# A hybrid mixer and MoE step on one core: another order in the first norm, four modulation sums moved, additions handed to GpSimd

## The chip, the cores and the metric

The kernel runs on one core of a Trainium2 chip. The metric is the device time of one execution in microseconds, lower is better. TensorE multiplies matrices, VectorE and ScalarE work on tiles elementwise, GpSimd does a few elementwise operations and issues some DMAs, SyncE issues most DMAs. In the profile they are PE (its weight loads: PEld), DVE, ACT, POOL and SP.

## The reference, cut to what matters

One layer for 128 context tokens and 1024 latent tokens of width 1024, all in fp32:

```python
mod = silu(c) @ w_mod + b_mod                 # 6 vectors of 1024, for context and latent each
shift1, scale1, gate1, shift2, scale2, gate2 = split(mod, 6)
hn = rmsnorm(x, norm1) * (1 + scale1) + shift1
u = hn @ w_in                                 # p (512), v (1024), g1 (1024), g2 (1024)
y_pool = pool_mixer(p)                        # 4 windows, one 128x128 product each
v = conv4(v)                                  # along the tokens
r, i = sigmoid(v @ w_r + b_r), sigmoid(v @ w_i + b_i)   # 2 directions, 16 heads of 64
a = exp(-8 * r * softplus(-lam)); h = scan(a * h + sqrt(1 - a^2) * i * v)
y_lru = h_forward + h_backward
merged = sigmoid(g1) * (y_pool @ w_br_pool) + sigmoid(g2) * (y_lru @ w_br_lru)
x = x + gate1 * (merged @ w_out)
x = x + gate2 * moe(rmsnorm(x, norm2) * (1 + scale2) + shift2)   # 16 experts, expert choice
y = rmsnorm(x, final_g)
```

## The kernel before

The program is written out by hand in one order (`manual_schedule`); each engine gets its instructions in the order in which the Python code emits them, and waits are set where tiles depend on each other. Products of fp32 matrices are done in halves: `split` (L181) copies a weight into `hi` in a rounded format on ScalarE (L188) and takes the remainder `lo` on VectorE (L189), and `mm3` (L197) adds three products on TensorE. A product of a 1024x128 block of `w_in` with all 1152 tokens (`dense`, L280) is 72 matmuls into one of two PSUM tiles.

**The list.** All weights of the first part stand in one list `seq` (L221 to L236): 18 items of the head, then v(2), g2(2), ... with one modulation sum m(n) behind each item, 28 in all, and bl(0) to bl(7) at the end. Behind v(7) come g1(0), g2(7), p(0) to p(3). `do_split(n)` (L269) splits the items up to number n that are not split yet and issues the loads some items further ahead; there are four buffers for `hi` and `lo` each and three for raw weights.

**The head.** The tokens are normalised, transposed, and modulated by scale1 and shift1, one channel block k of eight after the other. The modulation's first 2048 columns come in 16 blocks a(0) to a(15), four to a quarter q. `mod_first` multiplies one block; the blocks in `DP` are multiplied as plain fp32 with the vectors in `sil4`, the others in halves. `mod_low` copies a quarter's sums out of PSUM, `mod_second` transposes them by small products (L401) and adds the bias (L405). `hn_first(k)` and `hn_cols(k)`, `hn_low(k)` modulate block k and split it (L354 to L370), and `dense_v(j, k)` multiplies it for v(0) and v(1) at once.

**The gates.** For each j, `conv(j)` convolves v on VectorE, `gates(j)` does the four gate products of 9 matmuls (TensorE) with a Sigmoid each (ScalarE), `gates_rest(j)` is a chain of Tanh, Exp, Square, Sqrt on ScalarE and products on VectorE, and `scans(j)` does the scans and their split on VectorE. In the main loop (L722) an item v(j) is followed by its `gates(j - 1)`, `conv(j)`, a `do_split(i + 5)` and `gates_rest(j - 1)`. The last of them hang on g1(0): its product, its Sigmoid (`gate_evac`), `scans(6)`, `gates(7)`, `do_split(i + 5)`, and `gates_rest(7)` behind the next m. In this way the order at the end of the gates is, with what is split at each place:

```
v(7) m10 gates(6) conv(7) [split g2(7)] gates_rest(6)
g1(0) scans(6) gates(7) [split m12, p(0)] m11 gates_rest(7) [split m13]
g2(7) scans(7) ...
```

**The modulation sums.** `mod_block` (L660) does the 8 products of one m(n) into a PSUM tile that two neighbours share; behind the second, ScalarE copies it (L669), and five items later `mod_cols` (L209) transposes it on TensorE (L213) and adds on VectorE (L217, L218). Such postponed steps are in `later` and are taken at the head of the loop, ahead of the item's product. The transposes and sums take turns in two PSUM tiles.

**The pooling.** `pool_evac(g)` (L609) copies p(g) out of PSUM on ScalarE, calls `pool_mm(g - 1)` and does a chain of additions on VectorE.

**The projection.** `project(i, h)` (L955) multiplies tile i of 128 tokens with half h of `w_out`; VectorE multiplies by gate1 (L980) and adds the input rows (L981), which SyncE loads into a tile of two in turn, behind the norm's stores in its queue. Then come the second norm (`norm2`, L1005), the router, and steps of the routing (`affinities`, `first_cols`, `first_row`, `part_ranks`, `prompt_b`) hung on given products. After that the 16 experts' weights are streamed.

Of the kernel before, what the change touches and what calls it, by code (L numbers as in the profile page):

```python
# [8 lines left out]
F32 = mybir.dt.float32  # L9
# [17 lines left out]
FL, FM = 0, 0  # L27
DP = range(4)
T = SP + SL
# [20 lines left out]
def hybrid_step_kernel(ctx: ExitStack, tc: tile.TileContext, x_prompt, x_sample, state_lru, c, c_ctx,  # L50
# [69 lines left out]
    pk = const.tile([P, 16], F32, name="pk")  # L120
    l_a = ini.tile([P, 16], F32, name="l_a")
    l_e = ini.tile([P, 16], F32, name="l_e")
    l_z = ini.tile([P, 16], F32, name="l_z")
    l_q = ini.tile([P, 16], F32, name="l_q")

# [103 lines left out]
    full = [("v", 0), ("v", 1), ("g2", 0), ("g2", 1)]  # L229
    for n, jb in enumerate(seq[4:]):  # L230
        full.append(jb)
        if n < 32 - 2 * NGT:
            full.append(("m", n))

# [116 lines left out]

    def hn_cols(k):
        for x, z in ((xv[:, k, 0, :SP], 0), (xv[:, k, 0, SP:], 1), (xv[:, k, 1:], 1)):
            V.tensor_scalar(x, x, s1[:, z, k:k + 1], modc[:, 0, z, k:k + 1], op0=OP.mult, op1=OP.add)  # L354
        A.copy(hn_hi[:, k, :].rearrange("p (g t) -> p g t", g=3), xv[:, k])

# [36 lines left out]
    def mod_low(q):  # L393
        mrow1[q] = xsp.tile([P, D], F32, name="mrow1", tag="junk")[:4, :512]
        A.copy(mrow1[q][:, :256], mps[q][:4, :256])
        (A.copy if q else V.tensor_copy)(mrow1[q][:, 256:], mps[q][:4, 256:])

# [30 lines left out]
    go1(slice(6, 9))  # L428
    do_split(4)
    norm1(2)  # L430
    x_cols1(1, 0, A)
    x_cols1(1, 1, A)
    mod_first(0)
    mod_first(1)
    x_cols1(2, 0, V)
    x_cols1(2, 1, A)
    mod_first(2)
    mod_first(3)
    mod_low(0)
    do_split(5)  # L440
    mod_second(0)
    turn[0] += FL
    va = [acc_tile(), acc_tile()]
    hn_first(0)
    do_split(8)

    for q in range(4):
        k = 2 * q
        if q < 3:
            do_split(4 * q + 10)  # L450
        dense_v(0, k)
        for n in (4, 5) if q < 3 else ():
            mod_first(4 * q + n)
        hn_cols(k + 1)
        dense_v(1, k)
        for n in (6, 7) if q < 3 else ():
            mod_first(4 * q + n)
        hn_low(k + 1)
        if q < 3:
            mod_low(q + 1)  # L460
            do_split(4 * q + 12 if q < 2 else HEAD + 2)
        dense_v(0, k + 1)
        if q < 3:
            mod_second(q + 1)
        dense_v(1, k + 1)
        if q < 3:
            hn_first(k + 2)
    softplus()
    do_split(HEAD + 2)
# [17 lines left out]
    G.memset(graw, 0.0)  # L487
    LR = {}

    def load_gates(j):  # L490
# [118 lines left out]
    def pool_evac(g, a3):  # L609
# [5 lines left out]
        for q in range(2):  # L615
            A.copy(lat[:, 4 + 6 * q:10 + 6 * q], a3[:, 1 + q, :CH].rearrange("p (r c) -> p r c", c=GW))
        if g:
            pool_mm(g - 1)
# [85 lines left out]
    later = []  # L704
    rests = []
    load_gates(0)
    v_evac(va[0])
    conv(0)
    for j in range(2):
        do_split(HEAD + 1 + j)  # L710
        a3 = dense(spl.pop(("g2", j)), KD, hn_hi, hn_lo)
        if j == 0:
            v_evac(va[1])
        A.dma_start(g2_d[j], gate_evac(a3))
        if j == 0:
            gates(0)
            conv(1)
            do_split(HEAD + 4)
            gates_rest(0)
        else:  # L720
            scans(0)
    for i in range(HEAD + 2, len(seq)):  # L722
        kind, j = seq[i]
        if kind == "m" and (kind, j) not in spl and i < done_split[0]:
            continue
        if (kind, j) != ("g1", 0):
            do_split(i + 4)
        for d in list(later):
            d[0] -= 1
            if d[0] <= 0:  # L730
                d[1]()
                later.remove(d)
        if kind == "bl" and j == 0:
            mg_hi = pool_sb["dp"].tile([P, KD, T], F32R, name="mg_hi", tag="D")
            mg_lo = big.tile([P, KD, T], F32R, name="mg_lo", tag="H2")
        if kind == "m":
            mod_block(j // 2, j % 2, spl.pop((kind, j)))
            for f in rests:
                f()
            rests = []  # L740
            if j == 31 - 2 * NGT:
                later.append([5, mod_rows])
            continue
# [15 lines left out]
        else:  # L759
            a3 = dense(w, KD, hn_hi, hn_lo)  # L760
        if kind == "g1" and j:
            g1s[j] = gate_evac(a3)
# [3 lines left out]
        if kind == "v":  # L766
            v_evac(a3)
            if seq[i + 1][0] == "m":
                n = seq[i + 1][1]
                mod_block(n // 2, n % 2, spl.pop(("m", n)))  # L770
            gates(j - 1)
# [7 lines left out]
        elif kind == "g1":  # L779
            if j == 0:  # L780
                g1s[j] = gate_evac(a3)
                scans(KD - 2)
                gates(KD - 1)
                do_split(i + 5)
                rests.append(lambda: gates_rest(KD - 1))
            if j == 3:
# [168 lines left out]
    def project(i, h, mid=(), part=False):  # L955
# [24 lines left out]
        V.tensor_tensor(tmp, ps, g1r[z][:, hs], op=OP.mult)  # L980
        V.tensor_tensor(x2s[i][:, hs], x2s[i][:, hs], tmp, op=OP.add)  # L981

# [814 lines left out]
```

## Time and profile before

| | |
|---|---|
| median of 3 runs | 2151.72 us (2150.81 to 2152.35) |
| profiled execution | 2155.95 us |
| its span, first to last instruction | 2154.2 us |
| TensorE busy | 2070.4 us (96%) |
| VectorE busy | 1709.6 us (79%) |
| ScalarE busy | 1358.8 us (63%) |
| GpSimd busy | 190.9 us (9%) |

Times in the profile's rows count from the span's start. A row of a timeline gives start, duration, engine, line, operation, output and inputs, and in brackets how long the engine was idle before and what released it. Matmuls overlap, so the distance of their starts is their cost.

### The profile page before, as it was taken

The page shows a single profiled execution, that of the slowest core. Times are in us where ns is not written, and L with a number is a line of the kernel's source. Part 1 is how long each engine was busy: PE and PEld are TensorE (multiplying, and loading weights), DVE is VectorE, ACT ScalarE, POOL GpSimd, SP SyncE. Part 2 cuts the span into 40 slices and gives each one's busy share as a digit, 9 for nine tenths or more (in the row PEclk, how much of TensorE's full clock was granted, in tenths as well). Part 3 has the DMA queues.
Part 4 walks back from the last instruction along what each step waited for, and adds up shares of the span by engine and source line. Part 5 has one row for each costly group of instructions (what it writes and reads, how often), then busy time and mean ns, then how long its engine had stood idle before and what let it go on. Part 6 is the DMA issues. An engine that isn't in the chain of part 4 may idle for free.

```text
span 2154.2 us, 40533 instructions
## 1 busy us (share of the span) xinstructions
PE 2070.4 (96%) x17269; PEld 1974.4 (92%) x17269; DVE 1709.6 (79%) x1847; ACT 1358.8 (63%) x1444; POOL 190.9 (9%) x324
## 2 busy tenths in 40 slices
PE   6999999999999987899999999999999999999995
PEld 4799998999998875899999999999999999999994
DVE  6788988732236467988988898998998998899896
ACT  6477675321112225677877777877877777777783
POOL 0000001010101001020010010011010011011021
PEclk9999999999999988999999999999999999999997
DMA  8133434174644238699999999999999999999995
GB/s 265 56 118 114 125 111 124 55 223 117 203 158 170 109 110 296 237 326 332 346 328 334 343 331 324 343 340 326 333 335 327 338 341 328 336 341 323 339 313 181
DMA packets 304820, 543.91 MB, mean 252 GB/s; under 512 B 16300, under 2 KB 85628, under 8 KB 304639
## 3 DMA queue, kind: packets, MB, share of 16 engines
q1 hardware_dynamic: 285306, 478.56, 64.0%
q0 software_dynamic: 15728, 52.77, 8.4%
q10 hardware_dynamic: 3604, 9.98, 1.4%
q8 instruction: 135, 2.21, 0.4%
q14 instruction: 47, 0.38, 0.1%
HBM read 500.60 MB, written 40.67 MB: 251 GB/s over the span
## 4 chain that ended last, share of the span: by engine, by line
PE 86%; DVE 8%; DMA 2%; ACT 2%; issue 1%; SPq 0%; DVEq 0%; ACTq 0%
PE ac L1465 37%; PE ac L1473 17%; PE a L198 6%; PE a L199 6%; PE a L200 6%; PE a L757 5%; DVE lo L1280 2%; PE a L984 1%; PE a L986 1%; PE a L985 1%; DMA xg<-hn_d,lgi 1%; PE tp L1404 1%; PE tp L1489 1%; DVE lo L189 1%; PE tp L665 1%
## 5 line engine op out<-in xcount | busy, mean ns | idle before, releaser
L1280 DVE TENSOR_TENSOR lo<-raw,hi 128x2048 bf16<-128x2048 f32 x384 | 870.9, 2281 | 0.0
L1274 ACT CAST hi<-raw 128x2048 fp32r<-128x2048 f32 x384 | 729.4, 1912 | 3.8 <-issue 2.2
L1465 PE MATMUL ac<-x,hi 128*128 128x288 f32 x4096 | 606.1, 300 | 0.0
L1465 PEld LDWEIGHTS ac<-x,hi 128*128 128x128 f32 x4096 | 553.0, 189 | 1.0 <-issue 0.9
L1473 PEld LDWEIGHTS <-lo 128*128 128x128 bf16 x6144 | 380.4, 98 | 36.7 <-DVE lo L1280 0.8
L1465 PE MATMUL ac<-hh,hi 128*128 128x288 f32 x2048 | 332.9, 304 | 0.0
L1478 ACT COPY bs<-ac 128x288 f32<-128x288 f32 x320 | 127.8, 399 | 290.6 <-PE ac L1473 289.1
L1473 PE MATMUL ac<-xb,lo 128*128 128x144 bf16 x4096 | 302.4, 227 | 0.6 <-DVE lo L1280 0.6
L1465 PEld LDWEIGHTS ac<-hh,hi 128*128 128x128 f32 x2048 | 279.9, 189 | 0.0
L198 PE MATMUL a<-hn_hi,hi 128*128 128x384 f32 x624 | 212.0, 340 | 0.0
L199 PE MATMUL a<-hn_lo,hi 128*128 128x384 f32 x624 | 210.8, 338 | 0.0
L200 PE MATMUL a<-hn_hi,lo 128*128 128x384 f32 x624 | 210.8, 338 | 0.0
L1473 PE MATMUL ac<-hb,lo 128*128 128x144 bf16 x2048 | 171.9, 227 | 0.0
L189 DVE TENSOR_TENSOR lo<-raw,hi 128x1024 fp32r<-128x1024 f32 (+1 forms) x76 | 86.7, 1163 | 78.8 <-ACT hi L188 78.2
L1479 DVE TENSOR_TENSOR h<-ac,bs 128x288 f32<-128x288 f32 x256 | 115.7, 452 | 42.1 <-ACT bs L1478 41.8
L198 PEld LDWEIGHTS a<-hn_hi,hi 128*128 128x128 f32 x624 | 117.1, 188 | 0.4
L199 PEld LDWEIGHTS a<-hn_lo,hi 128*128 128x128 f32 x624 | 117.2, 188 | 0.0
L200 PEld LDWEIGHTS a<-hn_hi,lo 128*128 128x128 f32 x624 | 117.2, 188 | 0.0
L1710 POOL TENSOR_TENSOR yps<-ot,modc 128x128 f32<-128x128 f32 x16 | 35.9, 2247 | 735.2 <-DVE ot L1479 735.2
L188 ACT CAST hi<-raw 128x1024 fp32r<-128x1024 f32 (+1 forms) x76 | 74.8, 1001 | 41.2 <-PE a L199 33.3
L1479 DVE TENSOR_TENSOR ot<-ac,bs 128x288 f32<-128x288 f32 x64 | 29.3, 457 | 69.7 <-ACT bs L1478 69.7
L699 ACT ACTIVATE sg<-a 128x1152 f32<-128x1152 f32 x16 | 18.1, 1134 | 82.4 <-PE a L200 82.3
(447 smaller groups left out, 2626.8 us busy)
## 6 DMA issues: line engine op xcount, KB each, us to landing
raw<-in_exp_w_dram SPq DMA_DIRECT2D x380, 1024.0 KB, 7.2
raw<-in_w_in_dram SPq DMA_DIRECT2D x28, 512.0 KB, 5.0
raw<-in_w_mod_dram SPq DMA_DIRECT2D x28, 512.0 KB, 5.3
araw<-in_w_mod_dram SPq DMA_DIRECT2D x18, 256.0 KB, 4.5
g_d<-sg ACTq DMA_DIRECT2D x8, 576.0 KB, 3.2
yh_d<-yh POOLq DMA_DIRECT2D x8, 576.0 KB, 3.1
yl_d<-yl POOLq DMA_DIRECT2D x8, 576.0 KB, 4.6
m_d<-sg POOLq DMA_DIRECT2D x8, 576.0 KB, 4.2
```

Of the source, the lines that this page charges most:

```text
L188: A.copy(h, raw)
L189: V.tensor_tensor(l, raw, h.bitcast(F32), op=OP.subtract)
L198: PE.matmul(out, whi, xhi, start=first, stop=False)
L199: PE.matmul(out, whi, xlo, start=False, stop=False)
L200: PE.matmul(out, wlo, xhi, start=False, stop=last)
L757: PE.matmul(a3[:, ch, :CH], w[:, k, :], y[:, k, cs], start=n == 0 and k == 0 and w is hi, stop=n == 1 and k == KD - 1 and w is ws[-1])
L1274: A.copy(hl[n][0], raw[n])
L1280: V.tensor_tensor(lo, r, hi.bitcast(F32), op=OP.subtract)
L1465: PE.matmul(a[:, r, :2 * S], w[0][:, k, c0 + r * P:c0 + (r + 1) * P], x2(kk), start=kk == first, stop=False)
L1473: PE.matmul(a[:, r, S:2 * S], w[1][:, k, c0 + r * P:c0 + (r + 1) * P], xb(kk), start=False, stop=kk == last)
L1478: A.copy(b, a[:, :, S:2 * S])
L1479: V.tensor_tensor(dst, a[:, :, :S], b, op=OP.add)
```

## The change

- **List.** Four modulation sums instead of one stand behind g1(0); the rest keep their order.
- **Head.** Block a(3) is done in halves. Some `do_split` calls move; `hn_cols` is cut into `hn_mod` and `hn_high`, and `hn_mod` goes ahead of the splits; `mod_low` is one copy on ScalarE, behind the next two splits. `softplus` moves behind `conv(0)`.
- **Main loop.** The position is in `at`, and `sums_next(n)` takes the next n sums from the list where it is called: behind a v's evacuation, inside `pool_evac` ahead of `pool_mm`, and four of them between `scans(6)` and `gates(7)`. `gates_rest(7)` follows `gates(7)` at once. Postponed steps are taken behind an item's product instead of ahead of it.
- **Projection.** The addition of tiles 1 to 7 is done on GpSimd.

```diff
@@ -25,7 +25,7 @@
 NGT = 2
 G0, G1, GX, G2 = 3, 8, 9, 15
 FL, FM = 0, 0
-DP = range(4)
+DP = range(3)
 T = SP + SL
 NT = T // P
 CH = 384
@@ -118,10 +118,6 @@
     lamc = col_a[:, IA["lam"]:IA["lam"] + 16]
     nk = const.tile([P, 16], F32, name="nk")
     pk = const.tile([P, 16], F32, name="pk")
-    l_a = ini.tile([P, 16], F32, name="l_a")
-    l_e = ini.tile([P, 16], F32, name="l_e")
-    l_z = ini.tile([P, 16], F32, name="l_z")
-    l_q = ini.tile([P, 16], F32, name="l_q")
 
     def softplus():
         A.activation(l_a, lamc, AF.Abs)
@@ -227,10 +223,13 @@
         seq += [("g1", j), ("bp", j)]
     seq += [("g1", 6), ("g1", 7), ("bp", 6), ("bp", 7)]
     full = [("v", 0), ("v", 1), ("g2", 0), ("g2", 1)]
-    for n, jb in enumerate(seq[4:]):
+    n = 0
+    for jb in seq[4:]:
         full.append(jb)
-        if n < 32 - 2 * NGT:
-            full.append(("m", n))
+        for _ in range(4 if jb == ("g1", 0) else 1):
+            if n < 32 - 2 * NGT:
+                full.append(("m", n))
+                n += 1
 
     head = [("a", n) for n in range(4)] + [("v", 0), ("v", 1)] + [("a", n) for n in range(4, 16)]
     seq = head + full[2:] + [("bl", j) for j in range(8)]
@@ -349,9 +348,11 @@
         PE.transpose(tpb[:, :n_b], par_b[:n_b], ident[:n_b, :n_b])
         V.tensor_copy(col_b[:, :n_b], tpb[:, :n_b])
 
-    def hn_cols(k):
+    def hn_mod(k):
         for x, z in ((xv[:, k, 0, :SP], 0), (xv[:, k, 0, SP:], 1), (xv[:, k, 1:], 1)):
             V.tensor_scalar(x, x, s1[:, z, k:k + 1], modc[:, 0, z, k:k + 1], op0=OP.mult, op1=OP.add)
+
+    def hn_high(k):
         A.copy(hn_hi[:, k, :].rearrange("p (g t) -> p g t", g=3), xv[:, k])
 
     def hn_first(k):
@@ -392,8 +393,7 @@
 
     def mod_low(q):
         mrow1[q] = xsp.tile([P, D], F32, name="mrow1", tag="junk")[:4, :512]
-        A.copy(mrow1[q][:, :256], mps[q][:4, :256])
-        (A.copy if q else V.tensor_copy)(mrow1[q][:, 256:], mps[q][:4, 256:])
+        A.copy(mrow1[q], mps[q][:4])
 
     def mod_second(q):
         t = tp_tile()
@@ -426,46 +426,48 @@
     sq1(7, 9)
     params()
     go1(slice(6, 9))
-    do_split(4)
+    do_split(3)
     norm1(2)
     x_cols1(1, 0, A)
     x_cols1(1, 1, A)
+    do_split(4)
     mod_first(0)
     mod_first(1)
     x_cols1(2, 0, V)
     x_cols1(2, 1, A)
     mod_first(2)
     mod_first(3)
+    do_split(6)
     mod_low(0)
-    do_split(5)
     mod_second(0)
     turn[0] += FL
     va = [acc_tile(), acc_tile()]
     hn_first(0)
+    hn_mod(1)
     do_split(8)
 
     for q in range(4):
         k = 2 * q
-        if q < 3:
-            do_split(4 * q + 10)
+        if q:
+            hn_mod(k + 1)
+        do_split(4 * q + 10 if q < 3 else HEAD + 2)
         dense_v(0, k)
         for n in (4, 5) if q < 3 else ():
             mod_first(4 * q + n)
-        hn_cols(k + 1)
+        hn_high(k + 1)
         dense_v(1, k)
         for n in (6, 7) if q < 3 else ():
             mod_first(4 * q + n)
         hn_low(k + 1)
         if q < 3:
+            do_split(min(4 * q + 12, HEAD))
             mod_low(q + 1)
-            do_split(4 * q + 12 if q < 2 else HEAD + 2)
         dense_v(0, k + 1)
         if q < 3:
             mod_second(q + 1)
         dense_v(1, k + 1)
         if q < 3:
             hn_first(k + 2)
-    softplus()
     do_split(HEAD + 2)
     spl.pop(("v", 0))
     spl.pop(("v", 1))
@@ -486,6 +488,7 @@
     graw = lp.tile([P, 4, P], F32, name="graw")
     G.memset(graw, 0.0)
     LR = {}
+    l_a, l_e, l_z, l_q = (lp.tile([P, 16], F32, name=f"l{n}") for n in "aezq")
 
     def load_gates(j):
         for m, w in enumerate((lru_wr, lru_wi)):
@@ -614,6 +617,7 @@
         A.copy(lat[:, 0:4], a3[:, 0, SP:CH].rearrange("p (r c) -> p r c", c=GW))
         for q in range(2):
             A.copy(lat[:, 4 + 6 * q:10 + 6 * q], a3[:, 1 + q, :CH].rearrange("p (r c) -> p r c", c=GW))
+        sums_next(1)
         if g:
             pool_mm(g - 1)
         cur, a, b = ppad, 0, PADT
@@ -702,10 +706,10 @@
     g1s = {}
     late = []
     later = []
-    rests = []
     load_gates(0)
     v_evac(va[0])
     conv(0)
+    softplus()
     for j in range(2):
         do_split(HEAD + 1 + j)
         a3 = dense(spl.pop(("g2", j)), KD, hn_hi, hn_lo)
@@ -719,25 +723,40 @@
             gates_rest(0)
         else:
             scans(0)
-    for i in range(HEAD + 2, len(seq)):
-        kind, j = seq[i]
-        if kind == "m" and (kind, j) not in spl and i < done_split[0]:
-            continue
-        if (kind, j) != ("g1", 0):
-            do_split(i + 4)
+
+    def turn_later():
         for d in list(later):
             d[0] -= 1
             if d[0] <= 0:
                 d[1]()
                 later.remove(d)
+
+    def sums_next(n):
+
+        while n and seq[at[0] + 1][0] == "m":
+            at[0] += 1
+            m = seq[at[0]][1]
+            do_split(at[0] + 1)
+            turn_later()
+            mod_block(m // 2, m % 2, spl.pop(("m", m)))
+            if m == 31 - 2 * NGT:
+                later.append([5, mod_rows])
+            n -= 1
+
+    at = [HEAD + 1]
+    while at[0] + 1 < len(seq):
+        at[0] += 1
+        i = at[0]
+        kind, j = seq[i]
+        if (kind, j) != ("g1", 0):
+            do_split(i + 4)
+        if kind == "m":
+            turn_later()
         if kind == "bl" and j == 0:
             mg_hi = pool_sb["dp"].tile([P, KD, T], F32R, name="mg_hi", tag="D")
             mg_lo = big.tile([P, KD, T], F32R, name="mg_lo", tag="H2")
         if kind == "m":
             mod_block(j // 2, j % 2, spl.pop((kind, j)))
-            for f in rests:
-                f()
-            rests = []
             if j == 31 - 2 * NGT:
                 later.append([5, mod_rows])
             continue
@@ -758,6 +777,7 @@
                                       stop=n == 1 and k == KD - 1 and w is ws[-1])
         else:
             a3 = dense(w, KD, hn_hi, hn_lo)
+        turn_later()
         if kind == "g1" and j:
             g1s[j] = gate_evac(a3)
         for f in late:
@@ -765,9 +785,7 @@
         late = []
         if kind == "v":
             v_evac(a3)
-            if seq[i + 1][0] == "m":
-                n = seq[i + 1][1]
-                mod_block(n // 2, n % 2, spl.pop(("m", n)))
+            sums_next(1)
             gates(j - 1)
             conv(j)
             do_split(i + 5)
@@ -780,9 +798,10 @@
             if j == 0:
                 g1s[j] = gate_evac(a3)
                 scans(KD - 2)
+                sums_next(4)
                 gates(KD - 1)
                 do_split(i + 5)
-                rests.append(lambda: gates_rest(KD - 1))
+                gates_rest(KD - 1)
             if j == 3:
                 ppk.close()
                 yhp = pyh.enter_context(tc.tile_pool(name="yhp", bufs=1, reuse_waits="tile"))
@@ -978,7 +997,7 @@
             return
         tmp = tk.tile([P, 512], F32, name="tmp", bufs=2)
         V.tensor_tensor(tmp, ps, g1r[z][:, hs], op=OP.mult)
-        V.tensor_tensor(x2s[i][:, hs], x2s[i][:, hs], tmp, op=OP.add)
+        (G if 0 < i < NT - 1 else V).tensor_tensor(x2s[i][:, hs], x2s[i][:, hs], tmp, op=OP.add)
 
     def mm3_t(out, xhi, xlo, whi, wlo, first, last):
         PE.matmul(out, xhi, whi, start=first, stop=False)
```

## Rows read from the trace of the kernel before

**Rows 1.** Cores; then the page's busy us (share) and instructions.
```profile
core 0: 2154.2 us, clock 0.983
...
PE 2070.4 (96%) x17269; PEld 1974.4 (92%) x17269; DVE 1709.6 (79%) x1847; ACT 1358.8 (63%) x1444; POOL 190.9 (9%) x324
```

**Rows 2.** Stretches: us, busy us by engine, granted clock, DMA share, GB/s.
```profile
769.00:775.00 6.00, 5.64 (x26) 4.85 (x27) 3.92 (x9) 2.08 (x3) 0.00 (x0) 0.72 0.30 105
...
780.00:792.00 12.00, 12.00 (x34) 9.41 (x34) 6.72 (x25) 2.81 (x4) 1.23 (x3) 0.51 0.11 44
...
792.00:803.00 11.00, 11.00 (x62) 9.45 (x61) 6.00 (x19) 4.26 (x7) 0.00 (x0) 1.00 0.42 145
```

**Rows 3.** TensorE's timeline: start, us, instruction, idle before, releaser.
```profile
324.12 0.61 PE L198 MATMUL a<-vhi,ghi 128*128 128x386 f32 x1 [2.63 <-ACT sg L699]
...
332.08 0.28 PE L665 MATMUL tp<-hi,cond 128*128 128x256 f32 x1
...
333.02 0.35 PE L198 MATMUL a<-hn_hi,hi 128*128 128x384 f32 x1
...
345.79 0.28 PE L213 MATMUL tp<-ident,mrow 4*128 4x4 f32 x2
...
362.88 0.25 PE L213 MATMUL tp<-ident,mrow 4*128 4x4 f32 x2 [2.06 <-DVE modc L218]
```

**Rows 4.** ScalarE's timeline, 318 to 400 us.
```profile
322.93 1.13 ACT L699 ACTIVATE sg<-a 128x1152 f32<-128x1152 f32 x1
...
335.35 0.35 ACT L669 COPY mrow<-tp 4x256 f32<-4x256 f32 x1
...
335.61 2.41 ACT L537 ACTIVATE lt<-gate,pk 128x1158 f32<-128x1158 f32 x2
...
345.78 2.24 ACT L547 ACTIVATE lt<-lt 128x1158 f32<-128x1158 f32 x2
...
347.92 1.04 ACT L188 CAST hi<-raw 128x1024 fp32r<-128x1024 f32 x1
```

**Rows 5.** VectorE's timeline, 318 to 400 us.
```profile
324.76 0.41 DVE L559 TENSOR_TENSOR_SCAN lt<-gate 128x128 f32<-128x128 f32 x1
...
332.82 1.23 DVE L568 TENSOR_TENSOR yl<-lt,yh 128x1024 fp32r<-128x1024 f32 x1
...
348.34 2.63 DVE L548 TENSOR_TENSOR gate<-gate,lt 128x1158 f32<-128x1158 f32 x2
...
350.89 1.22 DVE L189 TENSOR_TENSOR lo<-raw,hi 128x1024 fp32r<-128x1024 f32 x1
```

**Rows 6.** The head's timelines, and one group of its waits.
```profile
28.63 1.88 PE L386 MATMUL tp<-raw,sil 128*4 128x512 f32 x4
...
43.13 0.39 PE L389 MATMUL tp<-hi,cond 128*4 128x512 f32 x1
...
44.06 0.39 PE L389 MATMUL tp<-hi,cond 128*4 128x512 f32 x1
...
60.49 1.05 PE L401 MATMUL tp<-sum,mrow 4*128 4x2 f32 x8
...
62.37 0.16 DVE L405 TENSOR_TENSOR modc<-tp,col_b 128x8 f32<-128x8 f32 x1
...
PE a L199 <- DVE hn_lo L368: 2.6, 4, 1.0
```

**Rows 7.** The projection's timelines of TensorE and VectorE.
```profile
769.36 1.96 PE L1022 MATMUL tp<-rws,ht 128*128 128x16 f32 x16 [0.72 <-ACT ht L1016]
...
776.81 0.69 DVE L981 TENSOR_TENSOR sg<-sg,tmp 128x512 f32<-128x512 f32 x1 [3.68 <-issue]
...
779.20 1.19 PE L1092 MATMUL tp<-ident,cols 128*128 128x128 f32 x4 [3.44 <-DVE cols L1081]
```

**Rows 8.** Timelines of VectorE and GpSimd behind the projection.
```profile
807.37 1.03 DVE L156 TENSOR_TENSOR rq_b<-rq_b,rv_b 128x1 f32<-128x1 f32 x1
...
809.88 2.48 POOL L1343 TENSOR_TENSOR hn<-hn,t2r 128x512 f32<-128x512 f32 x2 [0.25 <-ACT hn L1331]
```

## The prediction

> **What bounds the kernel now.** I read the cores' row first: one core, 2154.2 us of span at a mean granted clock of 0.983. The page then shows TensorE busy for 96% of it [rows 1]. The experts' stage starts when the routing is done (about 815 us) and no edit touches its code, so what TensorE gains or loses ahead of it moves the end by as much. I therefore looked only for TensorE's idle time and half clock ahead of that, by stretches and then by its own timeline. Three places have some: the head (20 to 85 us), the last gates (320 to 363 us), the projection's end (768 to 792 us). In the stretches the column of the clock shows what a drop is: 780 to 792 us ran at 0.51, 1.2 GHz, and 792 to 803 us at 1.00, 2.4 GHz [rows 2]. Each engine's timeline shows one more thing that decides here: VectorE and ScalarE take their work in the order in which the program emits it. In the kernel before, the split of a weight emitted behind `gates_rest(7)` indeed runs only when that is done: ScalarE's copy at 347.92 behind the Sqrt of 345.78, VectorE's subtraction at 350.89 behind the products of 348.34 [rows 4, 5].
>
> **1. The head.** Block 3 of the modulation changes from plain fp32 on the fp32 weights (four passes from 28.63 on, pitch 0.43, 1.7 us) to split halves (four products, 43.13 to 44.06, 0.9 us) [rows 6]: -0.8. Its split, a copy of 1.04 and a subtraction of 1.22 us like the others [rows 4, 5], falls where both engines wait for transposes, so I cost it at nothing; without that cover it would cost its 2.3. The additions that follow `mod_second` are today queued behind subtractions: the transposing products start at 60.49 and last 1.05, the addition L405 starts at 62.37 and not at 61.5 [rows 6]. It is so four times in the head, three of them by about that much: with the splits ahead of `mod_low`, -2.5 in sum. `hn_mod` ahead of the splits takes away the waits of the odd quarters' low half, 2.6 us in four [rows 6], of which three, 1.6, go. The fourth grows: in the last pair the splits of the first two gate weights now stand before `hn_high(7)` and `hn_low(7)`, which puts two subtractions (2.4) into its chain; half of that I let fall into the wait for ScalarE that the chain has already: +1.2, and a wait near 3 us may drop the clock (waits of 2.63 and 3.44 did [rows 3, 7]), worth up to 2.4: half of it taken. Sum: -0.8 - 2.5 - 1.6 + 1.2 + 1.2 = -2.5; bounds -5.5 (the waits vanish, no drop) and 0. `softplus` behind `conv(0)` costs nothing: it is needed by `gates_rest(0)`, behind a product of 12.7 us; its 5 us would show only if that cover were gone.
>
> **2. The last gates.** This decides. `do_split(n)` splits items up to number n. In the old order, from v(7) on, come m10, g1(0), m11, g2(7); in the new one m10, g1(0), m11, m12, m13, m14, g2(7). The reach at `conv(7)` is unchanged (four items beyond v(7)), so it now ends with m12. g2(7) is no longer split there, and m13 and m14 are split by `sums_next` itself, one by one, behind `scans(6)`; g2(7) comes only in the loop's next turn, behind `gates_rest(7)`. Step by step, in the old trace's times:
> - The g1(0) product ends at 319.7. m11 takes 0.94 (332.08 to 333.02 [rows 3]). m12 takes over m10's and m11's PSUM tile, and its copy waits on ScalarE behind the Sigmoid of 322.93, 1.13 us long [rows 4]: m12 starts at 324.4 and, after the idle time, runs at half clock to 326.3.
> - m13's subtraction stands behind the scans on VectorE. They start at 324.76 and end with the subtraction of 332.82, at 334.05 [rows 5]; two small additions and the split (1.22): 335.6. m13 ends at 337.3. Its copy (0.35) precedes m14's split on ScalarE (1.04), then VectorE (1.22): 339.95. m14 ends at 341.6.
> - `gates(7)`: four groups of nine products at a pitch of 0.176 (72 products from 333.02 to 345.79), 6.3 us, and 1.3 more for half clock: 349.2. Before, they ended at 332.1.
> - The last gate's Sigmoid (1.2, as each Tanh): 350.5. `gates_rest(7)` on ScalarE from Tanh to the end of Sqrt is 335.61 to 347.9, and VectorE's last product ends at 350.9 [rows 4, 5]: 15.3 us behind Tanh's start, so 365.8. g2(7)'s subtraction: 367.0. TensorE has nothing else to do, as its next instruction is g2(7)'s product.
> - That product is 12.7 us (333.02 to 345.8 [rows 3]), and some 5 us of it at half clock, as after the wait that ended at 324.12 [rows 3], cost 2.3: 382.0. m15 and the transposes 1.2, p(0) 12.7, transposes and m16 1.2: p(1) starts at 397.1.
>
> Before, it started at 363.1, after the wait of 2.06 at 362.88 [rows 3], which the transposes behind the product take away and which is thereby counted. The new order has done three more sums by then, 3 x 0.94 = 2.8. So 397.1 - 363.1 - 2.8 = +31.2. In `pool_evac` the sum ahead of `pool_mm` delays the pooling chain of VectorE at the last group by 0.94, with less work in front of its product: +0.3, as some of it is covered. Taken: +31.5. Bounds: +28 if the clock never drops and the waits overlap more; +36 if the drops last as long as the one of 780 to 792 us.
>
> Nothing gives this back later: from 440 us to the projection's end TensorE shows no wait, and a late start is passed on. VectorE and ScalarE are idle while TensorE waits, but no product is ready earlier for it. The scans of 7 (9.3 us) start at about 370 and end under g2(7) and p(0).
>
> **3. The projection.** 14 additions of 128x512 move to GpSimd, whose additions of that size take 1.24 each (2.48 for two [rows 8]), against 0.69 on VectorE (776.81 [rows 7]). x2s is thus ready some 0.6 later, which the next tile's first 15 products (0.23 each, 3.4 us) hide; without them 0.6 per tile. What goes are VectorE's stops for the input rows: the addition of 776.81 waited 3.68 (the view names no releaser; its product was long there, so it is the DMA of the input rows), and with it the maximum, the exponential and the columns that TensorE waited for, 3.44 at 779.20 [rows 7]. With GpSimd waiting instead, VectorE goes on at 771.4 and the columns are there within 0.2 us of need: -3.2. The half clock behind it is 12.0 us at 0.51 [rows 2], which is 5.9 too long, less 0.7 for its products of one column, which need not go faster: -5.2. The earlier stop of 0.72 at 769.36 [rows 7] comes from `prompt_b` on VectorE ahead of the norm, which the rank comparisons pushed back; these start 1.9 us earlier without the wait for rows: -0.7, and 769 to 775 us at 0.72 [rows 2] gives (1 - 0.72) x 6 = -1.7. Sum -10.8. Behind GpSimd's waiting additions stand only the next additions, `constants` (the first addition, 1.2, is ahead of them) and `value_parts`, none of which TensorE waits for there; the load of the next rows is issued behind the norm's stores and moves with them. Bounds: -11.5 and -3.1 (third rival).
>
> GpSimd and VectorE do get in each other's way: under GpSimd's operations of 806 to 812 us a VectorE product of one column took 1.03 [rows 8]. The Trainium skill, "SBUF — State Buffer", section "SBUF: two separate sides", says that VectorE and GpSimd share a port pair that the first to start holds for a whole instruction, against VectorE operations with two SBUF inputs too. By that rule an addition can hold VectorE for 1.24; by the timeline above none meets the columns' chain (GpSimd's wait for rows lasts to about 774, the columns are done at 773.2).
>
> **The sum.** -2.5 + 31.5 - 10.8 = +18.2 us. The profiled execution took 2155.95 (span 2154.2 and 1.75 around it) and would take 2174.2; it lies 4.2 above the median of the runs, 2151.7, which gives 2169.9.
>
> **Rivals.** *The splits don't hold TensorE* (10%): the subtractions of m13, m14 and g2(7) run early enough, by an order other than the emitted one. Then the gap at 321 to 329 us, with its wait of 2.63 [rows 3], takes three more sums (-2.8), the wait of 2.06 goes, and the total is -2.5 - 4.9 - 10.8 = -18.2: 2133.5, faster. For it speaks that the gap is there; against it the order of [rows 4, 5]. It decides as soon as g2(7)'s subtraction ends before the last gates' products. *Only the scans hold it* (8%): g2(7) is split in time. Then 17.8 of wait and 2.3 of clock go: -1.9, 2149.8, no measurable change. *The projection keeps its half clock* (12%): an addition on GpSimd meets the two small operations ahead of the columns, twice 1.24, and the drop of 5.2 stays: -3.1 in place of -10.8, total +25.9, 2177.6, slower. For it speaks the 1.03 of [rows 8]; against it the distance of one microsecond above.
>
> **How the numbers follow.** My forecast has 70%: 2169.9. Its own range is 2163 to 2181: the bounds sum to +11 (-5.5 + 28 - 11.5) and +33 (0 + 36 - 3.1), the upper end a little inside since the three hardly meet. To hold 8 in 10 with the third rival I reach somewhat below, to 2157. 0.2%, 4.3 us, is about what a measurement can tell from no change. Slower by more: the forecast and the third rival, 82%. Within: the second, 7%. Faster: the first and what is left of the second, 11%.
>
> **What would show it.** TensorE idle from about 326 to 335 us waiting for VectorE's L189, and for 15 to 18 us between the last gates' products and g2(7)'s, released by the same line; ScalarE's split of g2(7) right behind the Sqrt; no wait of TensorE for L218 in the pooling stage. In the head, L405 starting within 0.2 us of L401's end and a wait near 3 us before the last pair's second product. In the projection, no wait for the columns of 4 to 6 and a clock of 1.00 there. I am wrong if g2(7)'s split stands ahead of `gates_rest(7)` on either engine, or if TensorE is idle less than 20 us between 320 and 370.

## The result, and the profile after

The changed kernel takes 2168.36 us (median of four runs, 2167.6 to 2170.03) against 2151.84 for the kernel before beside it: the ratio is 1.0081 [1.0067, 1.0095], slower by 16.5 us. The prediction was 2169.9. The profiled execution took 2168.91 with a span of 2167.1 at a mean clock of 0.979; it lies close to its median, while that of before lay 4.1 above its own, so the two profiles differ by 13.0 and the medians by 16.5.

In the changed kernel the split's copy is L184 and its subtraction L185 (before L188 and L189), a modulation sum L669 and L670, the copy of its row L673, the products L194 to L196, the transposes' additions L213 and L214, the gate's Sigmoid of g1(0) L703, the gates' L530, Tanh L540, Sqrt L550, the products behind it L551, the scans L562 with their own split up to L571, the projection's multiplication and addition L999 and L1000, and `first_row` L1111.

TensorE's timeline of the changed kernel around the last gates, every instruction with a wait in 318 to 372 us (start, us, instruction, idle before, releaser), then the first sum and the product of p(1) behind it:

```profile
321.10 0.39 PE L669 MATMUL tp<-hi,cond 128*128 128x256 f32 x1 [3.41 <-ACT mrow L673]
332.01 0.58 PE L670 MATMUL tp<-lo,cond 128*128 128x256 f32 x1 [9.03 <-DVE lo L185]
335.26 0.58 PE L669 MATMUL tp<-hi,cond 128*128 128x256 f32 x1 [1.40 <-ACT hi L184]
336.53 0.58 PE L670 MATMUL tp<-lo,cond 128*128 128x256 f32 x1 [0.68 <-DVE lo L185]
361.07 0.69 PE L194 MATMUL a<-hn_hi,hi 128*128 128x384 f32 x1 [14.58 <-ACT hi L184]
364.23 0.69 PE L196 MATMUL a<-hn_hi,lo 128*128 128x384 f32 x1 [2.15 <-DVE lo L185]
379.30 0.39 PE L669 MATMUL tp<-hi,cond 128*128 128x256 f32 x1
394.38 0.34 PE L194 MATMUL a<-hn_hi,hi 128*128 128x384 f32 x1
```

Six waits sum to 31.25 us, where before had the 2.63 and the 2.06 of [rows 3] and one of 1.49. The long ones name their cause: m13's low half (9.03), and g2(7)'s high and low half (14.58 and 2.15). The other engines' timelines show what these splits stood behind. VectorE:

```profile
321.24 0.42 DVE L562 TENSOR_TENSOR_SCAN lt<-gate 128x128 f32<-128x128 f32 x1
329.32 1.23 DVE L571 TENSOR_TENSOR yl<-lt,yh 128x1024 fp32r<-128x1024 f32 x1
330.73 1.23 DVE L185 TENSOR_TENSOR lo<-raw,hi 128x1024 fp32r<-128x1024 f32 x1
360.40 2.64 DVE L551 TENSOR_TENSOR gate<-gate,lt 128x1158 f32<-128x1158 f32 x2
362.95 3.49 DVE L185 TENSOR_TENSOR lo<-raw,hi 128x1024 fp32r<-128x1024 f32 x3
```

And ScalarE:

```profile
320.96 1.04 ACT L184 CAST hi<-raw 128x1024 fp32r<-128x1024 f32 x1
333.91 0.36 ACT L673 COPY mrow<-tp 4x256 f32<-4x256 f32 x1 [11.91 <-PE tp L670]
334.17 1.04 ACT L184 CAST hi<-raw 128x1024 fp32r<-128x1024 f32 x1
357.86 2.23 ACT L550 ACTIVATE lt<-lt 128x1158 f32<-128x1158 f32 x2
359.99 2.92 ACT L184 CAST hi<-raw 128x1024 fp32r<-128x1024 f32 x3
```

ScalarE had m13's high half at 322.0, but VectorE was in the scans of 6 from 321.24 to 330.46 and began the subtraction at 330.73. m14's copy stood behind the copy of m13's row, before which ScalarE was idle for 11.91, until m13 itself was done: a ring from TensorE through ScalarE and VectorE, in which each waits for the one before. And g2(7)'s copy runs behind the Sqrt, its subtraction behind L551, as `gates_rest(7)` is emitted ahead of it. That is [rows 4, 5] once more, now with TensorE waiting at the other end. The clock was at half for all of 331 to 342 and 360 to 369 us.

The head of the changed kernel: the transposing products L401 and the addition L405 of the first pair, the last pair's second product, and then the stretch of 78 to 90 us (columns as in [rows 2]):

```profile
31.25 1.05 PE L401 MATMUL tp<-sum,mrow 4*128 4x2 f32 x8 [1.05 <-ACT mrow L396]
32.34 0.17 DVE L405 TENSOR_TENSOR modc<-tp,col_b 128x8 f32<-128x8 f32 x1 [0.16 <-PE tp L401]
...
77.78 0.44 PE L195 MATMUL a<-hn_lo,vh 128*128 128x384 f32 x1 [1.91 <-DVE hn_lo L369]
```

```profile
78.00:90.00 12.00, 12.00 (x61) 12.00 (x61) 8.83 (x11) 5.38 (x10) 0.46 (x2) 0.86 0.08 21
```

L405 starts 0.04 behind the end of its transposes (31.25 + 1.05), and VectorE is idle before it and waits for them, here 0.16 and in the other three pairs 1.09 to 3.87. The wait of the last pair that took 0.95 before is now 1.91, and a part of the stretch behind it runs at half clock. In the projection the transposes of the columns of 4 to 6 (the row of [rows 7] with 3.44, here the one of 802.00) have no wait left (TensorE's timeline), and the stretches ahead of and behind them run at full clock:

```profile
781.86 1.05 PE L1111 MATMUL tp<-ident,cols 128*128 128x128 f32 x8
802.00 0.68 PE L1111 MATMUL tp<-ident,cols 128*128 128x128 f32 x4
820.12 0.38 PE L1111 MATMUL tp<-ident,col 128*128 128x128 f32 x2
```

```profile
792.00:803.00 11.00, 11.00 (x64) 9.26 (x63) 8.72 (x32) 4.11 (x8) 1.30 (x1) 1.00 0.36 132
803.00:815.00 12.00, 12.00 (x69) 10.20 (x68) 9.57 (x34) 4.97 (x8) 4.80 (x7) 1.00 0.14 57
```

The three rows of `first_row` are marks at which both kernels do the same. Before, the second stands at 779.20 [rows 7], the others here:

```profile
752.93 1.05 PE L1092 MATMUL tp<-ident,cols 128*128 128x128 f32 x8
...
803.15 0.38 PE L1092 MATMUL tp<-ident,col 128*128 128x128 f32 x2
```

The shift is +28.93 ahead of the columns of 4 to 6 and +16.97 behind them, so the projection gave back 11.96.

### The profile page after: what moved, and what is told of

Read it like the earlier page. It is cut to its first block, busy times and chain, and to the rows that moved or that the text cites. A ratio compares the mean times of both kernels' runs of the same rounds, so it can differ in the third digit from the quotient of the medians.

```text
span 2167.1 us, 40528 instructions
## 1 busy us (share of the span) xinstructions
PE 2068.5 (95%) x17269; PEld 1975.8 (91%) x17269; DVE 1702.8 (79%) x1833; ACT 1359.2 (63%) x1442; POOL 208.7 (10%) x338
## 4 chain that ended last, share of the span: by engine, by line
PE 88%; DVE 7%; ACT 2%; DMA 1%; issue 1%; SPq 0%; DVEq 0%; ACTq 0%; POOLq 0%
PE ac L1484 36%; PE ac L1492 17%; PE a L195 7%; PE a L196 6%; PE a L194 6%; PE a L776 5%; DVE lo L1299 2%; PE a L1003 2%; PE a L1005 2%; PE a L1004 2%; DMA xg<-hn_d,lgi 1%; PE tp L1041 1%; PE tp L1423 1%; PE tp L669 1%; PE tp L670 1%
## 5 line engine op out<-in xcount | busy, mean ns | idle before, releaser
L194 PE MATMUL a<-hn_hi,hi 128*128 128x384 f32 x624 | 212.4, 340 | 14.6 <-ACT hi L184 14.6
L196 PE MATMUL a<-hn_hi,lo 128*128 128x384 f32 x624 | 212.0, 340 | 2.2 <-DVE lo L185 2.2
L185 DVE TENSOR_TENSOR lo<-raw,hi 128x1024 fp32r<-128x1024 f32 (+1 forms) x77 | 88.0, 1165 | 72.0 <-ACT hi L184 71.9
L194 PEld LDWEIGHTS a<-hn_hi,hi 128*128 128x128 f32 x624 | 118.2, 189 | 15.2 <-ACT hi L184 14.9
L196 PEld LDWEIGHTS a<-hn_hi,lo 128*128 128x128 f32 x624 | 118.1, 189 | 2.7 <-DVE lo L185 2.7
L184 ACT CAST hi<-raw 128x1024 fp32r<-128x1024 f32 (+1 forms) x77 | 76.0, 1001 | 39.5 <-PE a L195 24.5
L703 ACT ACTIVATE sg<-a 128x1152 f32<-128x1152 f32 x16 | 18.2, 1135 | 94.3 <-PE a L196 94.2
```

The source lines that it names most:

```text
L184: A.copy(h, raw)
L185: V.tensor_tensor(l, raw, h.bitcast(F32), op=OP.subtract)
L194: PE.matmul(out, whi, xhi, start=first, stop=False)
L196: PE.matmul(out, wlo, xhi, start=False, stop=last)
```

## The experiments

Ratios stand against the kernel before in runs beside it on the same chip (medians 2151.62 to 2152.53), and a gain behind a ratio is taken from the ratio; the difference of the medians departs from it by up to 2 us. Shifts are those of a mark in the profiled executions against the profiled execution of before.

**e1: one line of the last gates.** The changed kernel with g2(7) split ahead of `gates_rest(7)`:

```
                 gates(KD - 1)
-                do_split(i + 5)
+                do_split(i + 6)
                 gates_rest(KD - 1)
```

> The kernel after, with g2(7) split ahead of gates_rest(7) instead of behind it (do_split(i + 6) in place of do_split(i + 5)). Theory (the place of the splits in the queues of ScalarE and VectorE holds TensorE): the wait of 14.6 + 2.2 us before g2(7) shrinks to some 3, but m15 and p(0) are still split behind gates_rest(7), and a wait of about 3 us comes up behind the product of g2(7). Net -10 to -13 us against the kernel after: 2155 to 2159. Rival (TensorE waits there for gates_rest's own results, or only the scans of 6 matter): no change, 2168.

2156.12 us (2153.77 to 2159.97), ratio 1.0019 [1.001, 1.0029]: this line alone is worth 12 to 13 us of a change that costs 16.5 in all. TensorE's waits in 340 to 372 us:

```profile
345.92 0.44 PE L194 MATMUL a<-hn_hi,hi 128*128 128x384 f32 x1 [2.31 <-ACT hi L184]
347.18 0.45 PE L196 MATMUL a<-hn_hi,lo 128*128 128x384 f32 x1 [0.64 <-DVE lo L185]
362.32 0.50 PE L670 MATMUL tp<-lo,cond 128*128 128x256 f32 x1 [2.07 <-DVE lo L185]
```

The 14.58 and 2.15 became 2.31 and 0.64. `gates_rest(7)` is now in front of m15's split instead, and as a product of 12.7 us lies in between, that costs 2.07.

**e2: one sum in place of four.** The changed kernel with the list as it was:

```
-        for _ in range(4 if jb == ("g1", 0) else 1):
+        for _ in range(1):
...
-                sums_next(4)
+                sums_next(1)
```

> The kernel after with one modulation sum behind g1(0) instead of four, and one taken ahead of the last gates; all else is kept. Theory: conv(7)'s splits reach g2(7) again, the whole loss of 31.5 us goes, m11 fits into the gap ahead of the gates (-0.9) and the transposes no longer wait (-2.1); with the head (-3.1) and the projection (-12.0) the time is 2133 to 2136. Rival (the loss comes from gates_rest(7) or the postponed steps, whose new order is kept here): 2150 or more.

2141.21 us (2138.15 to 2146.53), ratio 0.9954 [0.994, 0.9968]. The loss is gone, and the rival with it, but 5 us or more of the gain that was expected are missing. TensorE's timeline shows three of the reasons, and the stretch of 412 to 426 us a fourth:

```profile
356.83 0.44 PE L196 MATMUL a<-hn_hi,lo 128*128 128x384 f32 x1 [2.30 <-DVE lo L185]
...
370.96 0.39 PE L669 MATMUL tp<-hi,cond 128*128 128x256 f32 x1 [1.13 <-ACT mr L698]
...
418.61 0.41 PE L194 MATMUL a<-ph,pwh 128*128 128x384 f32 x1 [1.39 <-DVE ph L645]
```

```profile
412.00:426.00 14.00, 11.72 (x59) 11.17 (x58) 10.55 (x12) 4.85 (x6) 0.00 (x0) 0.88 0.26 75
```

The wait of 2.06 ahead of p(1) [rows 3] is not saved by moving the transposes: p(1)'s low half is late by 2.30 in their place. A sum inside `pool_evac` waits 1.13 for a PSUM tile that ScalarE copies first (L698); before had no such wait. And in the pooling the wait for `ph`, 0.44 before, is 1.39 and followed by (1 - 0.88) x 14 / 0.5 = 3.4 us at half clock.

**e3: the projection alone.** The kernel before with this line:

```
-        V.tensor_tensor(x2s[i][:, hs], x2s[i][:, hs], tmp, op=OP.add)
+        (G if 0 < i < NT - 1 else V).tensor_tensor(x2s[i][:, hs], x2s[i][:, hs], tmp, op=OP.add)
```

> The kernel before with nothing but the additions of tiles 1 to 7 on GpSimd. Theory: VectorE no longer stops for the input rows, the columns of tiles 4 to 6 are in time, the clock stays at 2.4 GHz to the end of the projection: -11 to -12 us, 2140. Rival (GpSimd and VectorE block each other, and the half clock of 780 to 792 us stays): -3 us, 2149.

2142.6 us (2140.01 to 2144.74), ratio 0.9958 [0.9946, 0.997], so -9.0, less than the -11 to -12 expected. The clock is 1.00 from 764 to 792 us and the wait for the columns is gone.

**e4: the head alone.** The kernel before with `DP = range(3)`, `hn_mod` and `hn_high`, `mod_low`'s one copy and the new order of the head; `softplus` stays in the head.

> The kernel before with nothing but the head's edits (block 3 in halves, hn_mod and the splits moved, one copy in mod_low; softplus stays). Theory: -4.9 us at the last pair of products, of which the drop of the clock behind it takes 1.5 back: -3.4, 2148.5. Rival (what the head gains is waited for again at the first gates): 2151.8.

2146.85 us (2144.05 to 2151.73), ratio 0.9983 [0.9973, 0.9993], so -3.7 (by the medians -5.7: the twelve runs fall into seven of 2144.05 to 2147.37 and five of 2150.38 to 2151.73, and the profiled one is the fastest). The first modulation sum starts 5.1 earlier than before. Its projection is that of before, and shows how much of what [rows 2, 7] show depends on the execution (TensorE's wait, and the stretch around it, behind which the clock is 1.00 to 792 us):

```profile
773.72 1.19 PE L1096 MATMUL tp<-ident,cols 128*128 128x128 f32 x4 [3.28 <-DVE cols L1085]
```

```profile
764.00:780.00 16.00, 12.68 (x49) 10.13 (x49) 7.43 (x22) 2.36 (x4) 2.28 (x5) 0.68 0.18 66
```

The same wait, 3.28 here and 3.44 there, but half clock for (1 - 0.68) x 16 / 0.5 = 10.2 us, where the profiled execution of before had 5.1 us by the same sum in 764 to 780 (clock 0.84) and 11.8 in 780 to 792 (0.51). e6 below has this projection too: there the wait is 4.88 and half clock lasts 6.9 us.

**e5: four sums, with their splits ahead of the scans.** The changed kernel with another order behind g1(0):

```
-                scans(KD - 2)
                 sums_next(4)
+                do_split(i + 6)
+                scans(KD - 2)
                 gates(KD - 1)
-                do_split(i + 5)
+                do_split(i + 8)
                 gates_rest(KD - 1)
```

> The changed kernel with all four sums kept, but the splits of m13, m14 and g2(7) emitted ahead of the scans of 6, and those of m15 and p(0) ahead of the seventh gates' rest. If the loss is only where the splits stand in VectorE's and ScalarE's order, the waits of 9.0 and 14.6 + 2.2 us and the half clock around them go and the time is 2138 to 2146 us. If four sums ahead of the last gates cost by themselves (the PSUM tile behind the Sigmoid, the gates' tiles behind later scans), it stays at 2150 or above, with TensorE waiting in the gates instead.

2145.52 us (2143.32 to 2148.02), ratio 0.9966 [0.9954, 0.9978], 22.8 below the changed kernel with the same four sums. What is left, in TensorE's timeline:

```profile
320.23 0.58 PE L669 MATMUL tp<-hi,cond 128*128 128x256 f32 x1 [3.43 <-ACT mrow L673]
325.37 0.39 PE L669 MATMUL tp<-hi,cond 128*128 128x256 f32 x1 [1.40 <-ACT hi L184]
326.63 0.40 PE L670 MATMUL tp<-lo,cond 128*128 128x256 f32 x1 [0.88 <-DVE lo L185]
365.92 0.58 PE L669 MATMUL tp<-hi,cond 128*128 128x256 f32 x1 [3.38 <-DVE modc L214]
```

No wait stands behind the scans of 6 or `gates_rest(7)` any more. The four sums still don't fill the gap ahead of the gates for nothing: they wait 5.7 us themselves (the PSUM tile behind g1(0)'s Sigmoid, and the ring through the copy of the row). The last row is the transposes' addition: VectorE reaches it only behind the scans of 7, as in the 2.06 of [rows 3]. It is faster than before only by its head and its projection: e7, with these and the old order, is faster yet.

**e6: the list and the sums alone.** The kernel before with all edits but those of the head and of the projection.

> The kernel before with the edits of the list and the sums alone (four sums ahead of the last gates, sums in the pooling, transposes behind a product, softplus behind the first convolution), without the head and without the projection. If the three parts add up, it is slower than before by the gates' 31.5 us less what the transposes give: 2180 to 2187 us. If the head or the projection has a share in the loss, it is 2175 or below.

2183.69 us (2180.45 to 2185.03), ratio 1.0144 [1.0129, 1.016], so +31.0. Its long waits are those of the changed kernel, to 0.5 us (TensorE's timeline; the third row is the projection's wait for its columns):

```profile
335.55 0.58 PE L666 MATMUL tp<-lo,cond 128*128 128x256 f32 x1 [9.49 <-DVE lo L185]
...
364.87 0.69 PE L194 MATMUL a<-hn_hi,hi 128*128 128x384 f32 x1 [14.58 <-ACT hi L184]
...
812.30 1.19 PE L1107 MATMUL tp<-ident,cols 128*128 128x128 f32 x4 [4.88 <-DVE cols L1096]
```

Around the last of these rows the clock is 0.92 from 797 to 813 us and 0.82 from 813 to 825, which makes (1 - 0.92) x 16 / 0.5 + (1 - 0.82) x 12 / 0.5 = 6.9 us at half clock.

**e7: head and projection, the order of the sums as before** (e3 and e4 together).

> The kernel before with the head's edits and GpSimd's additions alone, the order of the sums as before. If head (3.7 measured alone) and projection (9.0 to 9.9 alone) add up: 2138 to 2141 us. If both earn from the same cover, 2143 or above.

2138.1 us (2135.58 to 2142.36), ratio 0.9942 [0.9928, 0.9955]. The product of the two single ratios is 0.9983 x 0.9958 = 0.9941, and with e6's, 1.0144 x 0.9942 = 1.0085 against 1.0081 for the whole change. The three parts add up within some 2 us: by the medians e3 and e4 are -9.9 and -5.7, and e7 is -13.5.

**e8: one sum, and none inside the pooling.** e2 with one line less in `pool_evac`:

```
-        sums_next(1)
         if g:
             pool_mm(g - 1)
```

> The kernel with one sum in place of four (2141.2 us), and without the sum emitted inside the pooling's evacuation. If that sum delays the pooling chain of the last group so that TensorE waits 2.3 us there and falls to half clock at 412 to 426 us, this goes: 2137 to 2139 us and a granted clock of 1.00 there. If what that kernel lacks against its sum lies in the wait of 2.3 us for p(1)'s low half instead, it stays at 2141.

2136.54 us (2136.14 to 2137.16), ratio 0.993 [0.9916, 0.9943]. The wait for `ph` is 0.44 again, as before the change, and the stretch keeps its clock (TensorE's timeline, then the stretch):

```profile
417.05 0.41 PE L194 MATMUL a<-ph,pwh 128*128 128x384 f32 x1 [0.44 <-DVE ph L644]
```

```profile
412.00:426.00 14.00, 12.67 (x74) 12.12 (x73) 10.82 (x12) 5.25 (x6) 0.00 (x0) 1.00 0.29 80
```

**e9: the last pair.** e8 with the splits of g2(0) and g2(1) behind the last pair's halves:

```
-        do_split(4 * q + 10 if q < 3 else HEAD + 2)
+        if q < 3:
+            do_split(4 * q + 10)
```

> The kernel with one sum and none inside the pooling (2136.5 us), and the splits of g2(0) and g2(1) behind the last pair's halves in place of ahead of them. If those two subtractions are what the last pair's second product waits for, its wait of 1.9 us falls below 0.5, nothing is late behind them, and the time is 2133.5 to 2136.5 us. If the wait has another releaser (ScalarE's copy), it stays at 1.5 or more.

2135.64 us (2134.55 to 2137.61), ratio 0.9923 [0.9909, 0.9937]; it can't be told from e8 by its time. In the profile the wait of 1.9 is 0.96, as it was before the change, and so neither below 0.5 nor at 1.5 or more, as the two cases of the expectation had it: two subtractions stood in the chain and made half of the wait, and the other half was there without them. The first modulation sum is 1.4 earlier than in e8.

**e10: and p(1) split ahead of the scans of 7.** e9 with this line:

```
             else:
+                do_split(i + 5)
                 scans(j)
```

> The same, and p(1) is split ahead of the scans of 7. If the scans (9.3 us on VectorE) are what makes p(1)'s low half late, the wait of 2.3 us ahead of p(1) goes and the time is 2131.5 to 2135 us. If the pooling chain, which then starts later on VectorE, gives the 2.3 back as a longer wait in the pooling, it stays within 0.5 us of the run before it.

2134.36 us (2131.95 to 2134.77), ratio 0.9914 [0.9901, 0.9928], the fastest of all: 18 us below before, 34 below the change. The wait of 2.30 for p(1)'s low half is gone from TensorE's timeline; m14, a product later, waits 0.50 for the transposes' addition, and the wait for `ph` stays 0.44, so nothing is given back. By the intervals e8, e9 and e10 overlap; that the line does what it should rests on the wait.

## Why the prediction held, step by step

**The last gates** (predicted +31.2 by the start of p(1), and +0.3 in the pooling). p(1) starts at 394.38, before at 363.06: +31.3. The head brought everything 3.1 earlier there, and the three more sums (2.8) come back later, so the term measures 31.3 + 3.1 - 2.8 = 31.6 us; e6, in which the pooling's sum is included, gives +31.0 by its runs. Its steps hold as well, shifted by the 3.1: m12 was put at 324.4 and starts at 321.10 + 3.1 = 324.2; m13's low half at 335.6, it is 335.1; m14's at 339.95, it is 339.6; g2(7)'s at 367.0, it is 367.3; g2(7)'s end at 382.0, m15 starts at 382.4. What made the sum right was to follow emission order on all three engines, not the length of any one of them. One length was read wrong: half clock behind the wait that ended at 324.12 was taken as some 5 us and 2.3 of cost, but lasted 3.4 in before's trace and cost 1.7. Behind g2(7)'s wait, for which it was the price, it lasted from 364.23 to 369.4, so that the 2.3 came out by chance. Of the signs that were named, the wait for g2(7) was put down to VectorE's subtraction alone; 14.58 of its 16.7 us are put down to ScalarE's copy, 2.15 to the subtraction. e1, e5 and e2 tell the causes apart by their medians: the place of g2(7)'s split is worth 12, together with those of m13's and m14's behind the scans 23, and without the four sums 27.

**The pooling** cost 0.4 instead of 0.3 here: the shift is 31.3 - 2.8 = 28.5 at p(1), once the sums are even, and 28.93 ahead of the projection (29.0 predicted). That it was so little is luck. The wait for `ph` grew from 0.44 to 1.17, and the clock behind it stayed at 1.00; in e1 the same wait has half clock behind it. The changed kernel (TensorE's timeline, the stretch), then e1:

```profile
455.04 0.42 PE L194 MATMUL a<-ph,pwh 128*128 128x384 f32 x1 [1.17 <-DVE ph L645]
```

```profile
454.00:468.00 14.00, 12.08 (x73) 11.85 (x74) 9.90 (x13) 7.04 (x8) 0.53 (x1) 1.00 0.44 133
```

```profile
439.49 0.41 PE L194 MATMUL a<-ph,pwh 128*128 128x384 f32 x1 [1.18 <-DVE ph L645]
```

```profile
438.00:452.00 14.00, 11.93 (x64) 11.59 (x64) 8.32 (x12) 5.85 (x6) 0.00 (x0) 0.88 0.43 130
```

The drop is worth (1 - 0.88) x 14 = 1.7 us; e5 has it behind a wait of 1.18 as well, e6 has not. The prediction had priced the delay and no drop. In e2 the same line costs 3.8 between the profiles of e2 and e8: 0.95 of the wait for `ph`, 1.7 of clock, and the 1.13 of the sum's own wait.

**The head** (predicted -2.5). L405 of the last pair comes 5.9 earlier than before, where the terms ahead of the last pair sum to -4.9. The last pair was put at +1.2, and its wait grew by 0.96 (to 1.91, where the signs named a wait near 3). The clock drop was put at half of 2.4 and occurred in this profile: 0.86 over 78 to 90 us, (1 - 0.86) x 12 = 1.7. Left are -3.1 to -3.4 at the modulation sums. In the profiles of e1 to e8 that have this head, the clock of this stretch was 1.00 and the shift is -4.2 to -5.6, so the full gain without a drop, put at -3.7, was under-sized and reaches the bound of -5.5 that was given.

**The projection** (predicted -10.8). In the two profiles it is -11.96, and both the wait and the half clock went, as said. But by the runs e3 has -9.0 [-11.6, -6.5]. The step that was mis-sized is the half clock of [rows 2]: -5.2 and -1.7 came from one execution, in which it lasted 16.9 us, while e4 and e6 with the same code had 10.2 and 6.9. (The second part's sentence that TensorE shows no wait from 440 us to the projection's end leaves out the 0.72 and the 3.44 that the third part counts; nothing is added up from it.)

**The sum.** Right to 1.5 us, it was also lucky: the projection was over-sized by 1.8 (by the ratios), the head under-sized by 1.2, and the drop in the pooling did not come. Nor does this pair of profiles bear out that what TensorE gains or loses ahead of the experts moves the end by as much. The shift is 16.97 at the projection's last mark (803.15 to 820.12) but 13.57 here, in TensorE's timelines of before and of the changed kernel:

```profile
925.06 1.09 PE L1404 MATMUL tp<-ident,xg 128*128 128x128 f32 x8 [1.75 <-DMA xg<-hn_d,lgi]
```

```profile
938.63 1.09 PE L1423 MATMUL tp<-ident,xg 128*128 128x128 f32 x8 [1.32 <-DMA xg<-hn_d,lgi]
```

From the one mark to the other before takes 121.9 us, e4 and e6, which have its code there, 119.1 and 120.6, and the changed kernel 118.5. So the profiled execution of before lost time here too, beside the long half clock of its projection. How much each adds to the 4.1 by which it lies above its median isn't shown.

**The rivals.** That the splits don't hold TensorE, or only the scans do, is ruled out by the two long waits. But the price that the first rival gave to the change without that hold, -18.2, was too good: e2, with one sum ahead of the gates in place of four, reaches -9.9. The 2.06 ahead of p(1) was counted as gained and was not, as the next late thing, p(1)'s own split behind the scans of 7, stood right behind it, and the pooling took 3.8. The third rival, half clock kept by an addition on GpSimd, did not occur: in the profiles of e2, e3, e5, e7 and e8, which have these additions, the clock is 1.00 from 764 to 780 us.

**Which part could have earned.** Head and projection alone give 0.9942. The other edits lose with four sums ahead of the last gates, and with a sum inside the pooling; what remains of them in e8, with one sum ahead of the gates and none in the pooling, can't be told from e7.

## What to carry to other kernels

Where a program moves work of one engine, list what the move does to the order on the engines that feed it: here three cheap sums for TensorE pushed a weight's split, 2.3 us of VectorE and ScalarE, behind 15 us of elementwise work, and one changed count (how far ahead to split) was worth 12 us. Before counting a removed wait as gained, look what is late next behind it on the same engine. And price a clock drop with its spread over executions, not by the one that was profiled.

## What the chip showed unasked

**The same wait costs a clock drop in one execution and none in another.** e8 and e9 have the same code from 100 us to the end. Each waits 2.5 us in the last gates and 2.30 ahead of p(1)'s low half. e8, 318 to 332 us and the product behind the second wait:

```profile
318.00:332.00 14.00, 10.05 (x55) 9.69 (x56) 13.30 (x16) 9.82 (x11) 1.06 (x2) 1.00 0.21 72
```

```profile
357.53 0.44 PE L196 MATMUL a<-hn_hi,lo 128*128 128x384 f32 x1 [2.30 <-DVE lo L185]
```

And e9:

```profile
318.00:332.00 14.00, 11.33 (x54) 11.02 (x55) 11.85 (x15) 8.28 (x10) 1.06 (x2) 0.88 0.24 84
```

```profile
357.80 0.69 PE L196 MATMUL a<-hn_hi,lo 128*128 128x384 f32 x1 [2.30 <-DVE lo L185]
```

The granted clock is 1.00 and 0.88 in the stretch, and the product behind the second wait takes 0.44 and 0.69. e9 leads by 1.3 us ahead of both and trails by 1.8 behind them. The waits of 1.2 for `ph` and of 1.9 in the head, above, had a drop in some profiles and none in others. So a profile in which a wait of 1.2 to 2.6 us has no drop behind it doesn't show that it is free.

**An addition on GpSimd can hold VectorE to its end.** In the changed kernel one addition met a rank comparison that takes 0.35 elsewhere. GpSimd's and VectorE's timelines:

```profile
788.28 1.29 POOL L1000 TENSOR_TENSOR sg<-sg,tmp 128x512 f32<-128x512 f32 x1 [9.82 <-DMA sg<-in_x_sample_dram]
...
787.12 0.35 DVE L1133 SCALAR_TENSOR_TENSOR beat<-arow,lg,tri 128x128 bf16<-128x128 f32 x1
788.44 1.28 DVE L1133 SCALAR_TENSOR_TENSOR beat<-arow,lg,tri 128x128 bf16<-128x128 f32 x1
```

The comparison ends 0.15 us behind the addition, and takes 0.93 longer than alone. No product waited for it. Not every operation is held: VectorE's MAX8, which reads one tile, took 0.28 under the next addition (793.04 to 794.34) and 0.27 ahead of it. The Trainium skill, "SBUF — State Buffer", section "SBUF: two separate sides", gives the rule: the two engines share a port pair, which the one that starts first keeps for its whole instruction, also against a VectorE operation with two SBUF inputs. The trace agrees, with the 1.28 above. GpSimd's addition of 128x512 takes 1.29, 1.9 times VectorE's 0.69 [rows 7], and its waits for the input rows, of 9.7 to 11.9 us, now stand in its own timeline and no longer in VectorE's.
